# Weights of an input projection kept by column block instead of by half of the contraction, with B21 as the second of seven products

## The chip, the cores and the metric

The kernel runs on one core of a Trainium2 chip. The metric is the device time of one execution in microseconds (us). The kernel before takes 1280.05 us, the median of three runs (1279.63 to 1282.67).

## The reference, cut to what matters

The kernel is one step of a decoder layer with two branches (causal pooling and a Mamba-2 scan) that share one input projection. The change touches the making of this projection for the prompt:

```python
h = rmsnorm(x, norm_g) * (1 + scale[:, None]) + shift[:, None]   # 1024 x 1024
proj = h @ w_in
u_pool, z_pool, z_ssm, xbc, dt_raw, g_raw = jnp.split(proj, SPLITS, axis=-1)
...
xbc_c, conv_new = causal_conv(xbc, conv_buf, conv_w, conv_b)
dt = jax.nn.softplus(dt_raw.astype(jnp.float32) + dt_bias.astype(jnp.float32))
```

All inputs and outputs are 32-bit floats. w_in has 1024 rows, the contraction. dt_raw and one pair of the gates' column blocks are made apart, ahead of the rest; the other columns go through the code of the change.

## The kernel before, in words

**The tiling.** The columns of w_in are worked through in blocks of 128, two at a time. There are 31 such pairs. In 23 of them the two blocks are neighbours, in the other 8 they lie apart. A pair is a matrix product of a 1024-wide contraction with 256 columns, over 1024 tokens, and is done by one step of the Strassen-Winograd scheme: the contraction and the columns are cut in halves, so that the raw weights of a pair are four blocks of 512 x 128, held as tiles of 128 partitions x 512 numbers: B11 and B12 (upper half of the contraction, first and second column block), B21 and B22 (lower half). Seven products take the place of eight. Their weights are B11, B21, B22 and four combinations, in the names of the code:

- t3 = B22 - B12
- t2 = t3 + B11
- B12 - B11, written over B12
- t2 - B21, the weight of the seventh product (the change names it t4)

The operands on the side of the tokens (S1 to S4 and plain parts of h) are made once, before the pairs.

**High and low halves.** Each weight is split by `split` (L162) into a high half `whi`, which ScalarE copies with rounding (L165), and a low half `wlo`, which GpSimd subtracts (L168; VectorE in the very first pair). Both have four buffers. A product (`product`, L596) is 24 matmuls of 128 x 272: two halves of the tokens, three terms (high by high, high by low, low by high), four slices of the contraction. High halves of the weight are read in the first eight of twelve, the low half in the last four. A half of the tokens ends in a bank of TensorE's output (PSUM, tiles `mm` and `ps`), and VectorE or ScalarE empties it with the function given to `product` (lines 614, 619 and 646 are these: add to a running sum, put a result out, copy).

**The buffers.** The raw weights live in three buffers `rawA`. A pair takes two: the first load holds B11 and B12, the second B21 and B22, each 512 KB (L537). Where the column blocks lie apart, each half is brought by two loads of 256 KB (L540). t3 and t2 take two of three buffers `raw`, made by `raw_`. The differences run on VectorE but for t2 - B21, which GpSimd does; all have line 551, in `diff`.

**The order of the work.** `pair_w` (L529) issues the loads and makes the first weight (B11), and leaves the others to a generator `steps`. `run_units` calls it one pair ahead of its use. `between(n)` (L699) runs behind product n of a pair, counted from 0, and for n = 3, 4 and 5 it does the next of the three steps of the following pair: first t3, then t2 and its splits, then the rest. So most pairs have their weights ready before their first product. What is left of the steps when a pair starts is done at once (`run` in `pair`, L670). Three pairs stand out:

- The first pair has an order of its own (`first_steps`, `opening`), with B21 as second product already.
- The second pair starts right behind the first one, which has no `between`. All three steps of the second pair are run at its start.
- The last ten pairs are a second call of `run_units` (L1688). There is no pair ahead within that call, so the first of the ten also runs all its steps at its start. In that stretch `samples_beside` (L1651) lets the chain that makes dt run beside the products: dt goes out to DRAM, comes back as the tile s (L1080, on the SP queue) and is turned by TensorE (L1099). From there on the order of TensorE's instructions is that of the program.

The framework then orders the instructions of each engine by a simulated schedule with priorities; each engine runs its own in that order, and the queue of SP issues most loads in its order. A load waits in the SP queue until its buffer is free, and what is behind it waits too. Along with the pairs the queue stores scratch weights (`ws`, L438), and VectorE runs the convolution (`GA`, L1047).

```python
def fourth(s, p):
    out(d1, HF, u3, c2)(s, p)
    add(u2, u2)(s, p)
```

The running sums of a pair are s1, u2, u3 and the scratch c2, each with 2 x 272 numbers on a partition. `out` writes a finished quarter of the pair's result, with a buffer of that set as the place for it.

Of the kernel before, what the change touches and what calls it, by code (L numbers as in the profile page):

```python
# [8 lines left out]
F32 = mybir.dt.float32  # L9
# [11 lines left out]
P = 128  # L21
D = 1024
KT = D // P
# [18 lines left out]
HF, SB = T // 2, T // 4  # L42
# [4 lines left out]
def tile_pool_ssd_step(  # L47
# [6 lines left out]
    nc = tc.nc  # L54
    uid = [0]

    def nm(s):
        uid[0] += 1
        return f"{s}_{uid[0]}"
# [10 lines left out]
    def open_(name, bufs, side="left"):  # L70
        cm = tc.tile_pool(name=name, bufs=bufs, side=side, reuse_waits="tile")
        kept.append(cm)
        return cm.__enter__()
# [10 lines left out]
    pa = open_("pa", 1)  # L84
# [25 lines left out]
    load = nc.sync.dma_start  # L110
# [60 lines left out]
    def raw_(shape=(P, 4, P)):  # L171
        return pa.tile(list(shape), F32, tag="raw", name=nm("raw"), bufs=RAW)
# [291 lines left out]
    S2, S1, S3 = [None] * 4, [None] * 4, [None] * 4  # L464

    def a_part(i, j):
        sl = lambda s: slice(HF * i + SB * s, HF * i + SB * s + SB)
        return lambda k, s: (hh_[4 * j + k][:, sl(s)], hl_[4 * j + k][:, sl(s)])

    def s_part(lst):  # L470
        return lambda k, s: (lst[k][:, 0, SB * s:SB * s + SB], lst[k][:, 1, SB * s:SB * s + SB])
# [57 lines left out]
    def pair_w(c0, c1, pri, early):  # L529
        def run():  # L530
            with tc.high_priority(pri):
                raws = []
                for j in range(2):
                    r = pa.tile([P, 4, 2, P], F32, tag="rawA", name=nm("rawA"), bufs=3)
                    rows_ = w_in[0, j * 512:(j + 1) * 512]
                    if c1 == c0 + P:
                        load(r, rows_[:, c0:c0 + 2 * P].rearrange("(k p) (t c) -> p k t c", p=P, c=P))  # L537
                    else:
                        for t, c in enumerate((c0, c1)):
                            load(r[:, :, t], rows_[:, c:c + P].rearrange("(k p) c -> p k c", p=P))  # L540
                    raws.append(r)
            b11, b12, b21, b22 = raws[0][:, :, 0], raws[0][:, :, 1], raws[1][:, :, 0], raws[1][:, :, 1]
            w = []

            def add(x):
                with tc.high_priority(pri):
                    w.append(split(x, highs, eng=V if early else None))

            def diff(dst, x, y, op=ALU.subtract, eng=V):
                with tc.high_priority(pri):  # L550
                    eng.tensor_tensor(dst, x, y, op)  # L551

            def first_steps():
                t3, t2 = raw_(), raw_()
                diff(t3, b22, b12)
                diff(t2, t3, b11, ALU.add)
                yield
                add(b11)
                add(b21)
                diff(b21, t2, b21)  # L560
                yield
                add(b21)
                add(t2)
                yield
                add(t3)
                yield
                diff(b12, b12, b11)
                add(b12)
                yield
                add(b22)  # L570
                yield

            def steps():
                t3, t2 = raw_(), raw_()
                diff(t3, b22, b12)
                yield
                diff(t2, t3, b11, ALU.add)
                add(t2)
                add(t3)
                yield  # L580
                diff(b12, b12, b11)
                add(b12)
                add(b21)
                diff(t2, t2, b21, eng=nc.gpsimd)
                add(t2)
                add(b22)
                yield
            if early:
                return w, first_steps()
            add(b11)  # L590
            prep_q.append(steps())
            return w, prep_q[-1]
        return run
# [4 lines left out]
    def product(w, A, use):  # L598
        for s in range(2):
            turn[0] ^= 1  # L600
            p = (PA if turn[0] else PB)()[:, :SB]

            for j in range(12):
                k = j % 4
                mm(p, w[j // 8][:, k], A(k, s)[j // 4 == 1], start=(j == 0), stop=(j == 11))  # L605
            with tc.high_priority(PRI):
                use(s, p)

    def strassen(w, d0, d1, early=False):
        def tmp(tag):  # L610
            return pa.tile([P, 2, SB], F32, tag=tag, name=nm(tag))

        def add(x, y):
            return lambda s, p: V.tensor_tensor(y[:, s], x[:, s], p, ALU.add)  # L614

        def out(d, o, x, buf, op=ALU.add):
            def use(s, p):
                def put(dst, a=0, b=SB, v=lambda t: t):
                    V.tensor_tensor(dst, v(x[:, s, a:b]), v(p[:, a:b]), op)
                d(o + SB * s, SB, put, buf)  # L620
            return use

        def fourth(s, p):
            out(d1, HF, u3, c2)(s, p)
            add(u2, u2)(s, p)
        s1, u2, u3, c2 = tmp("s1"), tmp("u2"), tmp("u3"), tmp("c2")
        if early:
            def fifth(s, p):
                out(d0, HF, s1, u3, ALU.subtract)(s, u3[:, s])
                out(d1, HF, s1, c2)(s, p)  # L630
                add(u2, u2)(s, p)
            product(w[0], a_part(0, 0), lambda s, p: act(s1[:, s], p, AF.Copy))
            yield
            product(w[1], a_part(0, 1), out(d0, 0, s1, c2))
            yield
            product(w[2], a_part(1, 1), lambda s, p: act(u3[:, s], p, AF.Copy))
            yield
            product(w[3], s_part(S2), add(s1, u2))
            yield
            product(w[4], s_part(S3), add(u2, s1))  # L640
            yield
            product(w[5], s_part(S1), fifth)
            yield
            product(w[6], s4_part, out(d1, 0, u2, u2))
            return
        product(w[0], a_part(0, 0), lambda s, p: act(s1[:, s], p, AF.Copy))
        yield
        product(w[1], s_part(S2), add(s1, u2))
        yield
        product(w[2], s_part(S3), add(u2, u3))  # L650
        yield
        product(w[3], s_part(S1), fourth)
        yield
        product(w[4], a_part(0, 1), out(d0, 0, s1, s1))
        yield
        product(w[5], a_part(1, 1), out(d0, HF, u3, u3, ALU.subtract))
        yield
        product(w[6], s4_part, out(d1, 0, u2, u2))
# [1283 lines left out]
    for half in range(2):  # L1942
        c = slice(half * 512, half * 512 + 512)
# [32 lines left out]
    for i in range(8):  # L1976
# [4 lines left out]
        r = R((P, D))  # L1981
# [5 lines left out]
        out = y_prompt[0, i * P:(i + 1) * P, :]  # L1987
        for j, (c0, cw) in enumerate(cuts):
            s = slice(c0, c0 + cw)
# [57 lines left out]
```

## Time and profile before

| what | value |
|---|---|
| median of three runs | 1280.05 us (1279.63 to 1282.67) |
| the profiled execution's own time | 1281.91 us |
| its span, from the first to the last instruction | 1280.2 us |
| granted clock of TensorE, mean | 0.997 |
| busy: TensorE (PE) | 1255.5 us, 98% of the span |
| busy: VectorE (DVE), ScalarE (ACT), GpSimd (POOL) | 911.1, 657.0, 645.7 us |
| moved by DMA | 251.68 MB |

How to read the rows below. PE, DVE, ACT and POOL are the engines TensorE, VectorE, ScalarE and GpSimd; SPq is the DMA queue that SyncE issues. A row of the timeline has the start (us from the span's start), the length from there to the end of the group, the engine, the line of the program, the operation, `out<-in` by the program's names, the shapes, and xN for N instructions in a row; in brackets stands the idle time just before, with what ended it. A row of the windows has the stretch and its length, then for TensorE's matmuls, TensorE's weight loads, VectorE, ScalarE and GpSimd the number of instructions and the busy time, then the granted clock, the DMA share, and GB/s. A row of the waits has the waiting engine, tile and line, an arrow to what it waited for, and the sum, count and mean in us. A row of a tile has the engine, the operation, the count, the shortest, mean and longest duration in ns, and the stretch of the program. A row of a DMA queue has packets, MB and the share of the 16 DMA engines' time in the stretch.

### The profile page before, as it was taken

The numbers are of one execution on the slowest core, as the hardware profiler recorded it, in microseconds if no ns is written. First come the engines' busy times: TensorE is split into PE (matmuls) and PEld (weight loads), VectorE is DVE, ScalarE is ACT, GpSimd is POOL, SyncE is SP. The second block draws the span as 40 slices with busy tenths as digits, with TensorE's granted clock in tenths as the row PEclk, the third lists the DMA queues.
The fourth block names the chain that finished last, engine by engine and source line by source line (L and its number), as shares of the span: only waits on it lengthen the run. The fifth ranks groups of instructions, "written<-read, shape, count | busy, mean of one in ns | idle before, by whom it ended". The sixth has DMA issues, their size and how long they took to land.

```text
span 1280.2 us, 26308 instructions
## 1 busy us (share of the span) xinstructions
PE 1255.5 (98%) x9739; PEld 1172.3 (92%) x9739; DVE 911.1 (71%) x1635; ACT 657.0 (51%) x1508; POOL 645.7 (50%) x556
## 2 busy tenths in 40 slices
PE   7999999999999999999999999999999999999997
PEld 6779999999999999999999999989888889999786
DVE  4686678986989688776666665587766887579343
ACT  4665347465656555555656554655675756202111
POOL 1006659777868677554444444355666867300000
PEclk9999999999999999999999999999999999999999
DMA  9736354465456544444656564999769898675531
GB/s 332 244 118 210 121 172 155 152 209 186 135 170 209 160 151 147 136 162 126 179 166 197 158 192 143 336 323 299 229 216 277 271 297 261 211 265 183 210 107 50
DMA packets 232769, 251.68 MB, mean 197 GB/s; under 512 B 29729, under 2 KB 176881, under 8 KB 232634
## 3 DMA queue, kind: packets, MB, share of 16 engines
q1 hardware_dynamic: 160544, 171.60, 43.0%
q10 hardware_dynamic: 72098, 78.41, 18.0%
q8 instruction: 77, 1.26, 0.4%
q14 instruction: 50, 0.41, 0.1%
HBM read 167.06 MB, written 83.01 MB: 195 GB/s over the span
## 4 chain that ended last, share of the span: by engine, by line
PE 90%; DMA 3%; DVE 3%; ACT 2%; issue 2%; POOL 0%; ACTq 0%; SPq 0%; DVEq 0%; POOLq 0%
PE ps L605 23%; PE mm L605 23%; PE mm L358 19%; PE ps L1204 3%; PE ps L1993 2%; PE ps L1995 2%; PE ps L1994 2%; PE pc L1526 2%; PE ps L1207 2%; PE ps L233 2%; PE ps L1501 1%; PE ps L1294 1%; PE ps L1317 1%; DMA rawA<-in_w_in 1%; PE pc L1308 1%
## 5 line engine op out<-in xcount | busy, mean ns | idle before, releaser
L168 POOL TENSOR_TENSOR wlo<-rawA,whi 128x512 fp32r<-128x512 f32 x120 | 178.1, 1489 | 174.6 <-ACT whi L165 83.6
L168 POOL TENSOR_TENSOR wlo<-raw,whi 128x512 fp32r<-128x512 f32 x92 | 149.2, 1631 | 118.1 <-ACT whi L165 87.4
L358 PE MATMUL mm<-Y,whi 128*128 128x352 f32 (+1 forms) x960 | 197.0, 336 | 0.3 <-DVE Y L1564 0.3
L358 PEld LDWEIGHTS mm<-Y,whi 128*128 128x128 f32 x960 | 160.2, 189 | 6.5 <-issue 4.8
L605 PE MATMUL mm<-Y,whi 128*128 128x272 f32 x992 | 149.7, 293 | 2.2 <-ACT whi L165 2.2
L605 PE MATMUL ps<-Y,whi 128*128 128x272 f32 x992 | 145.7, 289 | 0.0
L605 PEld LDWEIGHTS mm<-Y,whi 128*128 128x128 f32 x992 | 133.5, 189 | 5.9 <-ACT whi L165 2.5
L605 PEld LDWEIGHTS ps<-Y,whi 128*128 128x128 f32 x992 | 132.7, 188 | 0.5 <-issue 0.4
L1047 DVE SCALAR_TENSOR_TENSOR GA<-GA,cvT,GA 128x1112 f32<-128x1112 f32 x72 | 129.2, 1798 | 0.4 <-ACT GA L1044 0.3
L165 ACT ACTIVATE whi<-rawA 128x512 fp32r<-128x512 f32 x125 | 78.3, 627 | 86.6 <-PE ps L605 55.8
L165 ACT ACTIVATE whi<-raw 128x512 fp32r<-128x512 f32 x96 | 58.5, 627 | 99.2 <-DVE raw L551 40.2
L358 PE MATMUL mm<-Y,wlo 128*128 128x352 f32 (+1 forms) x480 | 99.7, 329 | 0.0
L1192 ACT ACTIVATE dec<-dec,acT 128x128 f32<-128x128 f32 (+1 forms) x288 | 86.7, 383 | 23.1 <-POOL dec L1183 22.5
L605 PE MATMUL mm<-Y,wlo 128*128 128x272 f32 x496 | 84.2, 289 | 0.0
L605 PE MATMUL ps<-Y,wlo 128*128 128x272 f32 x496 | 82.7, 289 | 0.0
L358 PEld LDWEIGHTS mm<-Y,wlo 128*128 128x128 f32 x480 | 82.4, 189 | 0.1
L605 PE MATMUL mm<-G,whi 128*128 128x272 f32 x496 | 73.1, 290 | 1.2 <-DVE u L614 1.2
L605 PE MATMUL ps<-G,whi 128*128 128x272 f32 x496 | 72.7, 288 | 1.0 <-DVE u L614 1.0
L434 POOL TENSOR_TENSOR pw<-pw,ph 128x512 fp32r<-128x512 f32 x40 | 62.5, 1563 | 21.5 <-ACT ph L432 20.0
L605 PEld LDWEIGHTS mm<-Y,wlo 128*128 128x128 f32 x496 | 70.3, 188 | 0.4 <-POOL wlo L168 0.3
L605 PEld LDWEIGHTS ps<-Y,wlo 128*128 128x128 f32 x496 | 70.0, 188 | 0.0
L605 PEld LDWEIGHTS mm<-G,whi 128*128 128x128 f32 x496 | 66.5, 189 | 2.0 <-issue 1.3
(429 smaller groups left out, 2909.8 us busy)
## 6 DMA issues: line engine op xcount, KB each, us to landing
rawA<-in_w_in SPq DMA_DIRECT2D x46, 512.0 KB
dec<-acs_d SPq DMA_DIRECT2D x32, 512.0 KB
xbc<-GA ACTq DMA_DIRECT2D x24, 512.0 KB
rawA<-in_w_in SPq DMA_DIRECT2D x32, 256.0 KB
pw<-in_w_ssm_out ACTq DMA_DIRECT2D x32, 256.0 KB
ws<-ph ACTq DMA_DIRECT2D x32, 256.0 KB
ws<-pw SPq DMA_DIRECT2D x32, 256.0 KB
h<-in_state_ssm SPq DMA_DIRECT2D x32, 256.0 KB
```

The source lines that it names most:

```text
L165: ins = act(hi[:, :, :ncols], raw[:, :, :ncols], AF.Copy)
L168: (eng or nc.gpsimd).tensor_tensor(lo[:, :, :ncols], raw[:, :, :ncols], hi[:, :, :ncols].bitcast(F32), ALU.subtract)
L233: mm(px[:, c:c + n], xt[:n, k * P:(k + 1) * P], dg[0][:n, i * P:i * P + n], start=True, stop=True)
L358: mm(ps[:, :n], w[k // 4][h][:, k % 4, :], r[k][:, o:o + n], start=(j == 0), stop=(j == len(terms) - 1))
L434: nc.gpsimd.tensor_tensor(raw.bitcast(F32R), raw, hi.bitcast(F32), ALU.subtract)
L605: mm(p, w[j // 8][:, k], A(k, s)[j // 4 == 1], start=(j == 0), stop=(j == 11))
L1047: V.scalar_tensor_tensor(d[:, :n], rp[:, k:k + n], cvT[:, 24 * k + mc:24 * k + mc + 1], d[:, :n], ALU.mult, ALU.add)
L1192: act(dec[:, h], dec[:, h], AF.Exp, bias=acT[:S, c, 8 * g + h:8 * g + h + 1], scale=-1.0)
L1204: mm(o[hh], xd[:S, 2 * q + hh, :], dec[:S, 2 * q + hh], start=True, stop=state is None)
L1207: mm(o[hh], state[:, h * 64:h * 64 + 64], cE[:, h], start=False, stop=True)
L1526: mm(pu, bt, xw.rearrange("p h d -> p (h d)"), start=True, stop=True)
L1993: mm(ps[:, :cw], mhk, wo[k][0][:, s], start=(k == 0), stop=False)
```

## The change

It does three things.

- **Buffers by column block.** A buffer rawA now holds one column block over the whole contraction: the first B11 and B21, the second B12 and B22. There are two loads of 512 KB for every pair, also where the blocks lie apart, and each row of a load is a run of 128 numbers (512 bytes). Before, neighbouring blocks came in runs of 256 numbers.
- **The order of the products.** The products of every pair but the first were B11, t2, t3, B12 - B11, B21, B22, t2 - B21. They are now B11, B21, t2, t3, B12 - B11, B22, t4 = t2 - B21. The places of c2 and s1 in the running sums are exchanged to suit.
- **The steps.** The first step is t3 as before. The second makes t2, then the weights B21, t2 and t3 and the difference t4. The third makes B12 - B11 and its weight, and the weights t4 and B22. t4 has a buffer `raw` of its own, the third, where it was written over t2.

```diff
-                raws = []
-                for j in range(2):
-                    r = pa.tile([P, 4, 2, P], F32, tag="rawA", name=nm("rawA"), bufs=3)
-                    rows_ = w_in[0, j * 512:(j + 1) * 512]
-                    if c1 == c0 + P:
-                        load(r, rows_[:, c0:c0 + 2 * P].rearrange("(k p) (t c) -> p k t c", p=P, c=P))
-                    else:
-                        for t, c in enumerate((c0, c1)):
-                            load(r[:, :, t], rows_[:, c:c + P].rearrange("(k p) c -> p k c", p=P))
-                    raws.append(r)
-            b11, b12, b21, b22 = raws[0][:, :, 0], raws[0][:, :, 1], raws[1][:, :, 0], raws[1][:, :, 1]
+                cols = []
+                for c in (c0, c1):
+                    r = pa.tile([P, KT, P], F32, tag="rawA", name=nm("rawA"), bufs=3)
+                    load(r, w_in[0, :, c:c + P].rearrange("(k p) c -> p k c", p=P))
+                    cols.append(r)
+            (b11, b21), (b12, b22) = [(r[:, 0:4], r[:, 4:8]) for r in cols]
...
                 diff(t3, b22, b12)
                 yield
+
                 diff(t2, t3, b11, ALU.add)
+                t4 = raw_()
+                add(b21)
                 add(t2)
                 add(t3)
+                diff(t4, t2, b21, eng=nc.gpsimd)
                 yield
                 diff(b12, b12, b11)
                 add(b12)
-                add(b21)
-                diff(t2, t2, b21, eng=nc.gpsimd)
-                add(t2)
+                add(t4)
                 add(b22)
                 yield
...
         def fourth(s, p):
-            out(d1, HF, u3, c2)(s, p)
+            out(d1, HF, u3, s1)(s, p)
             add(u2, u2)(s, p)
...
-        product(w[1], s_part(S2), add(s1, u2))
-        yield
-        product(w[2], s_part(S3), add(u2, u3))
-        yield
-        product(w[3], s_part(S1), fourth)
-        yield
-        product(w[4], a_part(0, 1), out(d0, 0, s1, s1))
+        product(w[1], a_part(0, 1), out(d0, 0, s1, c2))
+        yield
+        product(w[2], s_part(S2), add(s1, u2))
+        yield
+        product(w[3], s_part(S3), add(u2, u3))
+        yield
+        product(w[4], s_part(S1), fourth)
         yield
```

Behind the change every line of the program stands three lines earlier, so that L165 and L168 stay and L605, L614, L619, L646, L1047, L1080 and L1099 become L602, L611, L616, L643, L1044, L1077 and L1096. The loads are then L535 and the differences L546.

How the instructions move on three engines, at the places that the prediction speaks of. A row has the line, the operation, and `out<-in` with the number of each buffer's use.

ScalarE where the second pair starts, before. rawA_1310 is B11 of the next pair, rawA_1302 the upper half of the second pair; raw_1325 is its t2 and raw_1324 its t3.

```order
L165 ACTIVATE whi_1316<-rawA_1310 128x512
L715 ACTIVATE u_133_1039<-u_133_1039 128x272
L646 ACTIVATE s_186_1354<-mm_1358 128x272
L432 ACTIVATE ph_1480<-pw_1386 128x512
L717 DMA z_166<-u_133_1039 128x544
L715 ACTIVATE c_134_1040<-c_134_1040 128x272
L433 DMA wp_178<-ph_1480 128x512
L717 DMA z_166<-c_134_1040 128x544
L715 ACTIVATE u_132_1038<-u_132_1038 128x272 x2
L165 ACTIVATE whi_1328<-raw_1325 128x512
L165 ACTIVATE whi_1332<-raw_1324 128x512
```

The same place now. rawA_1302 is the first column block of the second pair, and its copy in the second row is that of B21; raw_1323 is t2 and raw_1322 t3.

```order
L165 ACTIVATE whi_1314<-rawA_1310 128x512
L165 ACTIVATE whi_1327<-rawA_1302 128x512
L712 ACTIVATE u_133_1039<-u_133_1039 128x272
L643 ACTIVATE s_187_1353<-mm_1357 128x272
L432 ACTIVATE ph_1477<-pw_1385 128x512
L165 ACTIVATE whi_1331<-raw_1323 128x512
L714 DMA z_166<-u_133_1039 128x544
L712 ACTIVATE c_134_1040<-c_134_1040 128x272
L165 ACTIVATE whi_1335<-raw_1322 128x512
```

The copy for the second product (t2) stood nine rows behind that of the next pair's B11. The copy for the second product (now B21) stands right behind it, and that of t2 five rows behind.

VectorE at the same place, before. L484 makes the low halves of the tokens' operand Y for the last product of the first pair, L619 and L614 empty its banks.

```order
L168 TENSOR_TENSOR wlo_1222<-rawA_717,whi_1221 128x512
L484 TENSOR_TENSOR Y_486<-tf_323,Y_485 128x544
L484 TENSOR_TENSOR Y_486<-tf_328,Y_485 128x544
L619 TENSOR_TENSOR u_133_1039<-s_131_1037,u_133_1039 128x272
L619 TENSOR_TENSOR c_134_1040<-s_131_1037,mm_1229 128x272
L614 TENSOR_TENSOR u_132_1038<-u_132_1038,mm_1229 128x272
L619 TENSOR_TENSOR u_133_1039<-s_131_1037,u_133_1039 128x272
L619 TENSOR_TENSOR c_134_1040<-s_131_1037,ps_1247 128x272
L614 TENSOR_TENSOR u_132_1038<-u_132_1038,ps_1247 128x272
L551 TENSOR_TENSOR raw_1324<-rawA_1304,rawA_1302 128x512
```

And now:

```order
L168 TENSOR_TENSOR wlo_1222<-rawA_717,whi_1221 128x512
L546 TENSOR_TENSOR raw_1322<-rawA_1304 128x512
L484 TENSOR_TENSOR Y_486<-tf_323,Y_485 128x544
L484 TENSOR_TENSOR Y_486<-tf_328,Y_485 128x544
L616 TENSOR_TENSOR u_133_1039<-s_131_1037,u_133_1039 128x272
```

The difference t3 of the second pair has moved from behind the six operations on the banks to ahead of the last two low halves of Y.

The SP queue where the last ten pairs start, before. rawA_7472 and rawA_7474 are the two loads of the first of the ten, rawA_7480 and rawA_7482 those of the next pair.

```order
L438 DMA ws_214<-pw_6728 128x512
L438 DMA ws_215<-pw_6865 128x512
L537 DMA rawA_7472<-in_w_in 128x4x256
L438 DMA ws_216<-pw_7040 128x512
L438 DMA ws_217<-pw_7177 128x512
L537 DMA rawA_7474<-in_w_in 128x4x256
L537 DMA rawA_7480<-in_w_in 128x4x256
L537 DMA rawA_7482<-in_w_in 128x4x256
L1080 DMA s_7466<-dts_d 128x1024
```

And now, where rawA_7476 and rawA_7478 are the first of the ten:

```order
L438 DMA ws_214<-pw_6727 128x512
L438 DMA ws_215<-pw_6868 128x512
L438 DMA ws_216<-pw_7040 128x512
L535 DMA rawA_7476<-in_w_in 128x8x128
L438 DMA ws_217<-pw_7181 128x512
L535 DMA rawA_7478<-in_w_in 128x8x128
L535 DMA rawA_7484<-in_w_in 128x8x128
L535 DMA rawA_7486<-in_w_in 128x8x128
L1077 DMA s_7470<-dts_d 128x1024
```

The first load has changed places with one store of scratch; the second load stands behind the same stores as before, and the load of s behind the same loads.

## The prediction

> **What bounds the kernel now.** I read the page first: busy times, and the chain of waits that ended last.
>
> ```profile
> span 1280.2 us, 26308 instructions
> ...
> PE 1255.5 (98%) x9739; PEld 1172.3 (92%) x9739; DVE 911.1 (71%) x1635; ACT 657.0 (51%) x1508; POOL 645.7 (50%) x556
> ...
> PE 90%; DMA 3%; DVE 3%; ACT 2%; issue 2%; POOL 0%; ACTq 0%; SPq 0%; DVEq 0%; POOLq 0%
> ```
>
> TensorE is busy for 1255.5 of 1280.2 us and makes up 90% of the chain. The change adds and removes no matmul, so it can only win or lose TensorE's idle time, 24.7 us in the whole program. The pairs of column blocks, which the change touches, run from about 80 to 815 us. The windows and TensorE's waits in that stretch:
>
> ```profile
> 120.00:500.00 380.00, 380.00 (x2978) 373.86 (x2978) 306.88 (x470) 210.13 (x498) 281.51 (x173) 1.00 0.52 166
> ```
>
> ```profile
> PE mm L605 <- ACT whi L165: 2.2, 1, 2.2
> PE ps L1099 <- DMA s<-dts_d: 1.6, 1, 1.6
> PE mm L605 <- DVE u L614: 1.2, 1, 1.2
> PE ps L605 <- DVE u L614: 1.0, 1, 1.0
> PE ps L1317 <- ACT s L646: 0.9, 2, 0.6
> PE ps L1264 <- DVE u L614: 0.4, 1, 0.4
> ```
>
> From 120 to 500 us TensorE never stops: 2978 matmuls in 380 us, 127.6 ns each, so a product (24 matmuls) is about 3.1 us. All recorded waits of the stretch are 2.2 + 1.6 + 1.2 + 1.0 + 0.9 + 0.4 = 7.3 us. That is the most that the change can give. The first four, 6.0 us, stand at two places: where the second pair starts, and where the last ten pairs start. Exactly there a pair's weights are made all at once just before use, not a pair ahead. I then read the timeline at both.
>
> **The second pair (99 to 108 us).** The timeline, all engines:
>
> ```profile
> 99.50 2.46 DVE L484 TENSOR_TENSOR Y<-tf,Y 128x544 fp32r<-128x544 f32 x2
> ...
> 102.03 0.37 PE L605 MATMUL mm<-Y,whi 128*128 128x272 f32 x1
> ...
> 103.17 0.61 ACT L165 ACTIVATE whi<-rawA 128x512 fp32r<-128x512 f32 x1
> ...
> 103.98 1.79 DVE L551 TENSOR_TENSOR raw<-rawA,rawA 128x512 f32<-128x512 f32 x1
> ...
> 107.48 1.15 ACT L165 ACTIVATE whi<-raw 128x512 fp32r<-128x512 f32 x2 [0.56 <-DVE raw L551]
> 108.17 1.27 PE L605 MATMUL mm<-Y,whi 128*128 128x272 f32 x8 [2.24 <-ACT whi L165]
> ```
>
> The second product of this pair takes t2, which needs two differences on VectorE; the first starts at 103.98, and the copy whi comes at 107.48. TensorE waits 2.24 us for it. In the change the second product takes B21, which needs no difference. Its copy stands in ScalarE's order right behind the copy of 103.17 (the next pair's b11), so it would be there at 103.17 + 0.61 + 0.61 = 104.4, about 1.5 us before TensorE asks at 108.17 - 2.24 = 105.9. The third product (t2) is asked for a product later. **Term 1: -2.24 us.** What would be late next is that copy at 103.17: it waits for a load issued at 99.6, now one of 512 KB and not two of 256 KB. A load of 512 KB was released 4.04 us after its issue in the case below (531.41 to 535.45), so 103.65 instead of 103.17, inside the 1.5 us.
>
> Something is given back here. In VectorE's order the first difference now stands ahead of the two subtractions of 99.50 (L484), the low halves that the last product of the first pair reads. They end at 101.96 and the matmul of 102.03 starts at once: no slack. Durations of such operations:
>
> ```profile
> L168 POOL TENSOR_TENSOR wlo<-rawA,whi x120: 1267/1297/2379, 99.6 to 802.5; 128x512 fp32r<-128x512 f32 x120
> ...
> L551 DVE TENSOR_TENSOR raw<-rawA,rawA x31: 677/1337/2346, 50.2 to 783.2; 128x512 f32<-128x512 f32 x31
> ...
> L551 POOL TENSOR_TENSOR raw<-raw,rawA x30: 1280/1332/2383, 112.0 to 792.1; 128x512 f32<-128x512 f32 x30
> ```
>
> A difference takes 0.68 us undisturbed and 1.79 us in the slow case seen at 103.98. VectorE has to do the two low halves either way, and they already ran slowly there (2.46 for two), so I take the undisturbed price. **Term 2: +0.7 us, between 0 and 1.8.** On this the Trainium skill, "SBUF — State Buffer", section "Who interferes with whom", says that a VectorE instruction with two SBUF inputs and a GpSimd instruction that reads SBUF exclude each other for a whole instruction. The row's 677 against 2346 ns agrees. By that rule one GpSimd instruction of 1.3 us is in the way of the whole block once, as before, which gives the same +0.7.
>
> **The last ten pairs (522 to 562 us).**
>
> ```profile
> 522.54 1.77 DVE L551 TENSOR_TENSOR rawA<-rawA 128x512 f32<-128x512 f32 x1
> ...
> 528.90 0.42 DVE L614 TENSOR_TENSOR u<-s,mm 128x272 f32<-128x272 f32 x1
> ...
> 530.09 2.54 POOL L168 TENSOR_TENSOR wlo<-rawA,whi 128x512 fp32r<-128x512 f32 x2
> ...
> 531.41 4.14 SPq L537 DMA_DIRECT2D rawA<-in_w_in  x2
> ...
> 535.45 1.75 DVE L551 TENSOR_TENSOR raw<-rawA,rawA 128x512 f32<-128x512 f32 x1 [6.13 <-DMA rawA<-in_w_in]
> ...
> 537.13 0.42 DVE L614 TENSOR_TENSOR u<-s,ps 128x272 f32<-128x272 f32 x1
> 537.61 1.28 PE L605 MATMUL ps<-G,whi 128*128 128x272 f32 x8 [1.02 <-DVE u L614]
> ...
> 540.54 1.23 PE L605 MATMUL mm<-G,whi 128*128 128x272 f32 x8 [1.15 <-DVE u L614]
> ```
>
> VectorE stands 6.13 us before a difference whose operand is still being loaded. The load is late because its buffer holds the previous pair's upper half, B11 and B12. It is free only when GpSimd has made the low half of B12 - B11 (530.09), which is the fourth weight and waits for the pair before to end. Behind VectorE's wait stand the operations that empty TensorE's banks (537.13), and TensorE loses 1.02 + 1.15 us.
>
> In the change the second load of a pair takes the buffer of the previous pair's first column. B11 and B21 are used up by the difference of 522.54, the second copy and one subtraction on GpSimd, all in the steps behind the fifth and sixth product of the pair before. So the load can go at 522.54 + 1.77 = 524.3, or when the SP queue has stored the scratch that is ahead of it in both orders. With 4.04 us it lands at 528.4, when VectorE gets there (528.9, less one operation of 0.42 that now comes later). What is late next: all three differences now stand together ahead of the two operations that empty the banks, 3 x 0.68 to 3 x 1.79, 2.0 to 5.4 us. The bank of 537.61 was wanted at 537.61 - 1.02 = 536.6; the change has emptied it by 528.5 + 5.4 + 2 x 0.42 = 534.7 at the latest. **Term 3: -2.17 us.**
>
> The same queue holds the third place:
>
> ```profile
> 554.93 0.37 SPq L537 DMA_DIRECT2D rawA<-in_w_in  x1
> ...
> 555.47 0.38 SPq L1080 DMA_DIRECT2D s<-dts_d  x1
> ...
> 559.10 0.66 PE L605 MATMUL mm<-G,whi 128*128 128x272 f32 x4
> 561.31 1.09 PE L1099 MATMUL ps<-ident,s 128*128 128x128 f32 x8 [1.56 <-DMA s<-dts_d]
> ```
>
> The load s is queued behind the next pair's second load, which again waits for a buffer until 554.93. In the change that buffer is free after the copy and low half of B21, the second weight and not the fourth: two products, about 6 us, sooner. TensorE reaches L1099 only some 1 us sooner by its order. **Term 4: -1.56 us, between -1.56 and 0.**
>
> **What costs nothing.** The loads: all are now 512 KB in runs of 512 bytes, where 46 of them had runs of 1 KB. The same amount in both forms, from the DMA view of one stretch of 3.6 us and one of 3.8 us:
>
> ```profile
> q1 hardware_dynamic: 1056, 0.52, 52.4%
> ```
>
> ```profile
> q1 hardware_dynamic: 528, 0.52, 47.0%
> ```
>
> That is 0.524 x 16 x 3.6 = 30.2 us of engine time against 0.470 x 16 x 3.8 = 28.6, or 0.1 us per load over 16 engines. The DMA share in the windows row is 0.52, so it is hidden; uncovered it would cost 0.1 us at each of the two waited-for loads. The Trainium skill speaks against the change here: "DMA: Bandwidth & Descriptors", section "Why small descriptors are slow (HBM only)", gives a packet a fixed extra of about 3 cycles. By it 512 bytes cost 19 cycles and 1 KB 35, an estimate of 9% more, against 6% measured; the sum would be the same to 0.1 us. The eight pairs with columns apart issue two loads instead of four, and shorten the SP queue. Swapping c2 and s1 moves as many VectorE and ScalarE operations as before. The third piece of work per pair takes the third raw buffer; its owner in the next pair comes a whole pair later.
>
> The steady pairs: GpSimd's order was low halves of t2 and t3, then the subtraction; now it is low half of B21, subtraction, low half of t2. So t2's low half is put back by 2.6 to 4.8 us (one low half and one subtraction), and its product by 3.1: the margin changes by between +0.5 and -1.7 us. A pair of the heavy stretch:
>
> ```profile
> 411.06 3.97 POOL L168 TENSOR_TENSOR wlo<-raw,whi 128x512 fp32r<-128x512 f32 x2 [1.41 <-issue]
> ...
> 415.51 0.41 PE L605 MATMUL mm<-Y,wlo 128*128 128x272 f32 x2
> ```
>
> The first of the two is done by 413.4 and read at 415.51: 2.1 us of margin, more than 1.7. B21 no longer waits for VectorE either. Price taken: 0.
>
> **Sum.** -2.24 + 0.70 - 2.17 - 1.56 = -5.27 us. The profiled execution took 1281.91 us (span 1280.2), 1.86 above the median of the runs, 1280.05; its sum gives 1276.6. Taken off the median: 1274.8 us.
>
> **Rivals.** (1) The queue keeps it: SP gives the load s no earlier, because the copy of B21 itself sits late in ScalarE's order. Term 4 is 0: -3.7, 1276.3 us. Against it: the copy of B21 is now the second weight to be made, not the fifth; for it: ScalarE runs its queue in order. (2) The wait changes its place: the load of 524.3 is held by the scratch store ahead of it, and VectorE waits in front of its three differences. From a landing later than 536.6 - 0.84 - 5.4 = 530.4 on, TensorE waits again; at the old 535.45 terms 3 and 4 are gone: -1.5, 1278.5 us. (3) Slower: GpSimd. It is busy 281.51 of 380 us. If most of the 19 steady pairs up to 520 us have a margin under 1.2 us for t2's low half, not the 2.1 quoted, each loses about 0.5 us: +9.5 - 5.3 = +4.2, 1284.3 us. For it: GpSimd's long cases (2379 ns); against it: not one wait for wlo among TensorE's waits today.
>
> **How the numbers follow.** A measurement of this kernel tells about 0.3%, 3.8 us, from no change; faster is below 1276.2, slower above 1283.9. Forecast 0.50; rival 1 0.15; rival 2 0.23; rival 3 0.12. The forecast counts as faster nearly whole (0.48), and rival 1 sits at the bound, mostly inside (0.04 faster), which makes 0.52; rivals 1 and 2 with the forecast's remainder give 0.36 for the same; slower 0.12. All of the 7.3 us gone and term 2 at nothing gives 1272.8 as the low end. The high end is rival 2 with term 2 at 1.8 and a further 1 us, half the wait of term 3, behind the block of three: 1280.6. That leaves out rival 3 and little else.
>
> **What would show it.** Right: the waits of TensorE between 80 and 815 us lose the rows for ACT whi, DVE u and DMA s, and keep about 1.3 us; VectorE's 6.1 us for the load of rawA are gone; a new small wait or pause of 0.7 us stands near 102 us. Wrong: waits of TensorE for POOL wlo in the steady pairs (rival 3), VectorE waiting for rawA near 527 us (rival 2), or L1096 waiting for s (rival 1). A gain elsewhere than in these rows would make the argument wrong even at the right time.

## The result, and the profile after

The changed kernel takes 1290.67 us (median of 6 runs, 1289.49 to 1292.61) against 1280.68 us for the kernel before (median of 6). The ratio is 1.0075, with a 95% interval of 1.0062 to 1.0089: 10 us slower, where 5 us faster was forecast. In what follows, one execution of e11 that took 4936.75 us is left out of its ratio.

Three slips in the text above change no number of it. The weight t2 - B21 (t4) is the sixth of the seven and B22 the seventh, in both kernels. A row of a tile has the shortest, the median and the longest duration, not the mean. And a row of the waits has the sum, the count and the longest wait, not the mean.

The page of the changed kernel: its span and busy times.

```profile
span 1289.7 us, 26396 instructions
...
PE 1257.6 (98%) x9739; PEld 1172.6 (91%) x9739; DVE 925.9 (72%) x1635; ACT 657.8 (51%) x1508; POOL 645.2 (50%) x556
```

VectorE is busy 14.8 us longer (925.9 against 911.1) with the same 1635 instructions. TensorE's waits while the pairs run, from 80 to 815 us (sum, count, longest):

```profile
PE ps L1314 <- ACT s L643: 4.3, 2, 2.7
PE ps L806 <- DVE GA L790: 2.5, 1, 2.5
PE ps L1150 <- DVE wdT L1140: 1.3, 1, 1.3
PE ps L1201 <- DVE u L611: 1.3, 1, 1.3
PE ps L1263 <- DVE tn L1331: 1.3, 2, 0.6
PE ps L806 <- DVE u L611: 1.1, 1, 1.1
PE mm L602 <- DVE Y L484: 1.0, 2, 0.8
PE mm L602 <- DVE c L616: 0.9, 1, 0.9
PE ps L602 <- DVE GA L616: 0.4, 1, 0.4
```

Of the 7.3 us of before, the rows for ACT whi, DMA s and the two for DVE u in the products are gone, as forecast. But the rows now add up to 14.1 us, and 11.8 of these stand at other lines than the product's, where 2.9 us stood before (0.9 + 0.4 + 1.6): L806 is the product of the pooling branch, and L1150, L1201, L1263 and L1314 belong to the samples, whose work TensorE does between the products of the last ten pairs. The clock adds to this. Two windows of the changed kernel, behind the waits that end at 259.49 and at 751.01 us (the granted clock is the third number from the end):

```profile
260.00:264.00 4.00, 4.00 (x17) 3.40 (x17) 3.19 (x7) 3.87 (x9) 2.58 (x3) 0.57 0.44 109
752.00:755.00 3.00, 3.00 (x15) 3.00 (x15) 1.20 (x5) 0.00 (x0) 0.03 (x1) 0.50 0.75 238
```

It is 0.57 and 0.50 there. The clock record has it at a half for 3.41 us each time, from 260.20 and from 751.72 us on, which costs about 1.7 us twice. In the kernel before, no such stretch lies among the pairs; it has one behind them, at 1124.59 us, which the changed kernel's profile has not. Waits and clock of the pairs together: 14.1 - 7.3 + 3.4 = 10.2 us. Less 1.7 us for the later stretch that is gone, 8.5 us are left, against 9.5 us by which the span grew; 0.7 us of the rest is idle time of TensorE outside the pairs. So most of the loss lies in the pairs' stretch, and most of that in waits of TensorE's other work.

How two of these waits arise, from the timeline. In the eighth pair, ScalarE (first and second row) copies the weight t4, for which a buffer whi is free only when the second product has ended, ahead of the second half of s, the first product's result:

```profile
244.43 0.63 ACT L165 ACTIVATE whi<-raw 128x512 fp32r<-128x512 f32 x1 [0.97 <-PE ps L602]
244.97 0.38 ACT L643 ACTIVATE s<-ps 128x272 f32<-128x272 f32 x1
...
245.38 0.44 DVE L616 TENSOR_TENSOR GA<-s,ps 128x272 f32<-128x272 f32 x1 [3.46 <-ACT s L643]
...
256.02 1.24 DVE L789 TENSOR_TENSOR edge<-GA,rc 128x7 f32<-128x7 f32 x1
...
259.49 1.93 PE L806 MATMUL ps<-GA,pwt 128*128 128x256 f32 x4 [2.53 <-DVE GA L790]
```

VectorE needs s to empty the second product's banks, stands 3.46 us, and does not catch up before TensorE asks for the pooled rows at L806. On the way an operation on 7 numbers (L789) takes 1.24 us; e8 comes back to it. Among the samples, one chain of lateness goes through VectorE and ScalarE:

```profile
649.04 3.28 DVE L546 TENSOR_TENSOR rawA<-rawA,rawA 128x512 f32<-128x512 f32 x1
652.25 2.14 DVE L1317 SCALAR_TENSOR_TENSOR h<-h,E,ps 128x128 f32<-128x128 f32 x8
...
653.88 1.28 ACT L1189 ACT_TABLE_LOAD   x1 [2.78 <-DVE h L1317]
...
657.73 1.28 ACT L712 ACT_TABLE_LOAD   x1
659.03 0.75 ACT L712 ACTIVATE u<-u 128x272 f32<-128x272 f32 x2
659.68 0.38 ACT L643 ACTIVATE s<-mm 128x272 f32<-128x272 f32 x1
660.20 0.63 ACT L165 ACTIVATE whi<-rawA 128x512 fp32r<-128x512 f32 x1
660.73 0.38 ACT L643 ACTIVATE s<-ps 128x272 f32<-128x272 f32 x1
...
661.17 0.50 PE L1314 MATMUL ps<-dec 96*128 96x512 f32 x1 [2.68 <-ACT s L643]
```

The difference B12 - B11 takes 3.28 us, the states h come late, ScalarE stands 2.78 us for them, and the copy s, which would free the bank for L1314, stands behind a table load, sigmoids and a weight's copy.

### The profile page after: what moved, and what is told of

It reads as the page before. It is cut to its first block, busy times and chain, and to the rows that moved or that the text cites. A ratio compares the mean times of both kernels' runs of the same rounds, so it can differ in the third digit from the quotient of the medians.

```text
span 1289.7 us, 26396 instructions
## 1 busy us (share of the span) xinstructions
PE 1257.6 (98%) x9739; PEld 1172.6 (91%) x9739; DVE 925.9 (72%) x1635; ACT 657.8 (51%) x1508; POOL 645.2 (50%) x556
## 4 chain that ended last, share of the span: by engine, by line
PE 55%; DVE 4%; DMA 2%; issue 1%; ACT 1%; ACTq 0%; SPq 0%; POOL 0%; DVEq 0%; POOLq 0%
PE mm L358 18%; PE ps L602 9%; PE mm L602 9%; PE ps L1201 3%; PE ps L1990 2%; PE ps L1991 2%; PE ps L1992 2%; PE pc L1523 2%; PE ps L1204 2%; PE ps L1498 1%; DVE GA L1044 1%; PE ps L1291 1%; PE ps L1314 1%; DMA bc<-xbc 1%; PE pc L1305 1%
## 5 line engine op out<-in xcount | busy, mean ns | idle before, releaser
L168 POOL TENSOR_TENSOR wlo<-rawA,whi 128x512 fp32r<-128x512 f32 x120 | 179.3, 1501 | 205.8 <-ACT whi L165 112.9
L168 POOL TENSOR_TENSOR wlo<-raw,whi 128x512 fp32r<-128x512 f32 x92 | 150.0, 1636 | 92.6 <-ACT whi L165 67.5
L602 PE MATMUL mm<-Y,whi 128*128 128x272 f32 x992 | 151.7, 294 | 1.1 <-DVE Y L484 1.0
L602 PE MATMUL ps<-Y,whi 128*128 128x272 f32 x992 | 145.7, 289 | 0.0
L602 PEld LDWEIGHTS mm<-Y,whi 128*128 128x128 f32 x992 | 133.8, 190 | 5.4 <-DVE Y L484 1.4
L602 PEld LDWEIGHTS ps<-Y,whi 128*128 128x128 f32 x992 | 132.7, 188 | 0.6 <-issue 0.4
L1044 DVE SCALAR_TENSOR_TENSOR GA<-GA,cvT,GA 128x1112 f32<-128x1112 f32 x72 | 127.1, 1770 | 0.1
L165 ACT ACTIVATE whi<-rawA 128x512 fp32r<-128x512 f32 x125 | 78.0, 627 | 81.9 <-PE ps L602 62.4
L165 ACT ACTIVATE whi<-raw 128x512 fp32r<-128x512 f32 x96 | 59.9, 626 | 93.2 <-PE ps L602 40.2
L602 PE MATMUL mm<-Y,wlo 128*128 128x272 f32 x496 | 82.8, 289 | 0.0
L602 PE MATMUL ps<-Y,wlo 128*128 128x272 f32 x496 | 82.7, 288 | 0.0
L434 POOL TENSOR_TENSOR pw<-pw,ph 128x512 fp32r<-128x512 f32 x40 | 67.7, 1692 | 17.5 <-ACT ph L432 17.4
L602 PE MATMUL mm<-G,whi 128*128 128x272 f32 x496 | 74.3, 291 | 0.0
L602 PE MATMUL ps<-G,whi 128*128 128x272 f32 x496 | 73.4, 291 | 0.4 <-DVE GA L616 0.4
L602 PEld LDWEIGHTS mm<-Y,wlo 128*128 128x128 f32 x496 | 70.0, 189 | 0.1
L602 PEld LDWEIGHTS ps<-Y,wlo 128*128 128x128 f32 x496 | 70.0, 188 | 0.0
L602 PEld LDWEIGHTS mm<-G,whi 128*128 128x128 f32 x496 | 67.2, 190 | 0.6
```

The lines of the kernel that those rows point to most:

```text
L165: ins = act(hi[:, :, :ncols], raw[:, :, :ncols], AF.Copy)
L168: (eng or nc.gpsimd).tensor_tensor(lo[:, :, :ncols], raw[:, :, :ncols], hi[:, :, :ncols].bitcast(F32), ALU.subtract)
L434: nc.gpsimd.tensor_tensor(raw.bitcast(F32R), raw, hi.bitcast(F32), ALU.subtract)
L1044: V.scalar_tensor_tensor(d[:, :n], rp[:, k:k + n], cvT[:, 24 * k + mc:24 * k + mc + 1], d[:, :n], ALU.mult, ALU.add)
```

## The experiments

Two theories were set against each other. **A:** the new order of the products costs the time, since it shifts the emptying of banks and the copies on ScalarE and VectorE for which TensorE's other work waits. **B:** the layout costs it, since VectorE's differences got slower (the three groups of L551 and L546 that write raw or rawA: 105.4 us before, 123.9 after). Kernels are compared by their ratio to runs of the kernel before that were made along with each.

**Each part alone.** e1 takes the loads of the changed kernel and leaves order and steps; e2 takes order and steps, and leaves the loads.

```diff
 e1: before with
-                raws = []  ...  load(r, rows_[:, c0:c0 + 2 * P]...)
+                cols = []  ...  load(r, w_in[0, :, c:c + P]...)
 e2: after with the loads of before
```

> Buffers by column block alone, with the old order of the products and the old steps. Theory A (the new order of the products costs the time: it moves the work that empties the banks and the copies on ScalarE): this kernel keeps the old order and should take 1277 to 1282 us, with the 2.2 us wait of TensorE for whi at the second pair still there and no new waits of 1 us or more in the side work of the last ten pairs. Theory B (the layout makes VectorE's differences slower, 123.9 us in all after against 105.4 before, and VectorE comes late everywhere): 1286 us or more, and the differences take about 120 us here too.

> The new order of the products and the new steps alone, with buffers by half of the contraction as before. Theory A (order): 1286 to 1292 us, with waits of TensorE for ScalarE's copy s in the last ten pairs as in the changed kernel (4.3 us there). Theory B (layout): 1275 to 1281 us, differences near 105 us on VectorE.

e1: 1284.27 us, ratio 1.0035 (1.0023 to 1.0047). e2: 1287.50 us, ratio 1.0065 (1.0052 to 1.0077). TensorE's waits in e2, the largest:

```profile
PE ps L1319 <- ACT s L648: 3.1, 2, 1.6
PE ps L1031 <- DVE u L621: 2.4, 2, 1.4
PE mm L607 <- DVE u L616: 1.5, 1, 1.5
PE ps L1155 <- DVE wdT L1145: 1.3, 1, 1.3
PE ps L1268 <- DVE tn L1336: 1.3, 2, 0.6
```

The order alone brings most of the loss, and three of the four waits in the samples' work (L1319, L1155 and L1268 are L1314, L1150 and L1263 of the changed kernel; L1201 has no counterpart here). The slow differences come with the order too: 117.3 us in e2 (37.3 + 39.8 + 40.2), 98.9 in e1. So theory B has the wrong cause for them. But A's number for e1 was missed: the layout costs 4.4 us in the old order by the medians (0.35%). VectorE's waits for loads in e1, and the same row of the changed kernel:

```profile
DVE raw L546 <- DMA rawA<-in_w_in: 15.9, 8, 4.9
```

```profile
DVE raw L546 <- DMA rawA<-in_w_in: 2.3, 2, 1.7
```

Before it was one wait of 6.1 us. With the old order, B21 is used up late, by the last subtraction on GpSimd, and now it holds the buffer that the next pair's second load needs. That reading is argued from the code and the rows; it was not tried by itself. Nor does it say where TensorE loses the time: in e1's profiled execution (1282.56 us) TensorE's waits among the pairs add up to 7.4 us, no more than the 7.3 us before, and one stretch at half clock (from 655.05 us, about 1.7 us lost) is the only other loss that it shows there. In the changed kernel that wait is small, and whether the layout adds to the loss there is not settled: 1.0065 and 1.0075 have overlapping intervals.

**Which engine is late.** e3 moves the copy s of the last ten pairs to VectorE, e5 that of all pairs but the first; e4 moves t4 to VectorE.

```diff
 e3: after with
-        product(w[0], a_part(0, 0), lambda s, p: act(s1[:, s], p, AF.Copy))
+        product(w[0], a_part(0, 0), (lambda s, p: V.tensor_copy(s1[:, s], p)) if late[0] else (lambda s, p: act(s1[:, s], p, AF.Copy)))
 e5: after with
+        product(w[0], a_part(0, 0), lambda s, p: V.tensor_copy(s1[:, s], p))
 e4: after with
-                diff(t4, t2, b21, eng=nc.gpsimd)
+                diff(t4, t2, b21)
```

> The changed kernel, with the first product of each of the last ten pairs copied out of its banks by VectorE and not by ScalarE. Theory A says the waits of 2.68 and 1.59 us before L1314, and the stretch of 3.4 us at half clock after the second (1.7 us), come from ScalarE's queue, in which the copy stands behind sigmoids, a table load and a weight's copy: they go, 6.0 us, and the time is 1284 to 1287 us. If VectorE is what is late everywhere (theory B), twenty more copies on it (20 x 0.4 us) make it the same or slower: 1290 to 1294 us.

> The changed kernel, with the difference t4 on VectorE and not on GpSimd. Theory B (VectorE's differences are held up by GpSimd's instructions on the same buffers): the 93 differences of before lose part of their 123.9 us and the time falls to 1288 us or less, though 30 differences of 0.7 us are added. Theory A: VectorE only gets more to do, 1290 to 1295 us.

> The changed kernel, with the first product of every pair but the very first copied by VectorE. TensorE's order is all but that of the changed kernel. Theory A: the wait of 2.5 us at 259 us, with the 3.4 us at half clock behind it, comes from one copy s on ScalarE that stands behind a weight's copy which waits for the end of the second product (VectorE then stands 3.46 us for s). It goes too: against the kernel with VectorE's copies in the last ten pairs only (1285.7 us) 2 to 4 us less, 1281 to 1284 us, and VectorE's waits for s (28 us in all) are gone. Theory B (VectorE's load): 42 copies of 0.43 us more, 18 us, on a VectorE that is 80% busy in the heavy pairs: 1287 us or more, with longer waits before the pooled product L806.

e3: 1285.72 us, ratio 1.0047 (1.0035 to 1.0059). That is 0.28%, about 3.6 us, less than the changed kernel by the ratios (4.95 us by the medians). TensorE's order in its trace is that of the changed kernel, row for row. Its waits from 560 to 815 us:

```profile
PE ps L1150 <- DVE wdT L1140: 1.3, 1, 1.3
PE ps L1263 <- DVE tn L1331: 1.2, 2, 0.6
PE ps L1201 <- DVE u L611: 1.2, 1, 1.2
```

The row for ACT s is gone and the others stand. So the copy's place in ScalarE's queue is what TensorE waits for there (e8, below, shows that VectorE's lateness has a part in it too). e4: 1292.81 us, 1.0107 (1.0092 to 1.0122): taking GpSimd's subtraction to VectorE makes it worse, as A said. e5: 1289.32 us, 1.0071 (1.0059 to 1.0083), a miss for A. The wait at the eighth pair fell from 2.53 to 0.92 us, but in an earlier pair the pooled product now waits 2.27 us, and L1201 waits 2.19 us: VectorE has no room for 40 copies more than in e3 (20 pairs of two; the 42 of the expectation is a miscount). In the heavy pairs VectorE's load counts as well as ScalarE's order.

**With no side work.** In e6 the samples' work is taken out from between the products and done in one block near the end of the ten pairs, in both kernels.

```diff
-        while made_[0] < (due[0] - FIRST) * 4 * SSTEPS / (7 * LAST - FIRST - SPARE):
+        while made_[0] < (4 * SSTEPS + 1 if due[0] >= 7 * LAST - SPARE else 0):
```

> The kernel before, with the side work of the samples taken out from between the products of the last ten pairs and done in one block near their end. It is the base of the next run: the seven pairs from the 24th to the 30th run with no side work between their products. All theories: TensorE has no wait over 0.3 us in those pairs; the whole time is longer, since the block waits for its own chain.

> The changed kernel with the same move. Theory A (the new order costs only where side work on TensorE waits for operations that the new order puts later on ScalarE and VectorE): from the start of the 24th pair to the start of the 29th it takes the same time as the kernel before with the same move, within 0.5 us. Rival C (the new order slows the pairs themselves, by banks emptied later or weights made later): it takes 2 us or more longer there too.

Windows of the two kernels with the move, first before, then after:

```profile
640.00:740.00 100.00, 100.00 (x799) 100.00 (x798) 42.43 (x84) 39.43 (x79) 49.91 (x38) 1.00 0.30 97
```

```profile
640.00:740.00 100.00, 100.00 (x799) 100.00 (x799) 44.86 (x78) 38.57 (x81) 49.69 (x38) 1.00 0.33 100
```

And the two as they were, in a stretch of 150 us, first before, then after:

```profile
600.00:750.00 150.00, 148.68 (x1338) 140.72 (x1337) 97.83 (x247) 90.03 (x192) 67.56 (x56) 1.00 0.60 178
```

```profile
600.00:750.00 150.00, 144.23 (x1288) 136.34 (x1286) 101.76 (x235) 85.72 (x184) 66.03 (x54) 1.00 0.58 167
```

Without side work both do 799 matmuls in 100 us and never stop. With it TensorE stands 1.3 us before and 5.8 us after. In these pairs the new order does not slow the products; it makes the side work between them wait. For the heavy pairs e6 shows nothing of the kind: the waits before L806 stand in it too (2.6 and 0.8 us), and so does the wait of 1.3 us before L1150, at 598 us. The whole times of these two runs (1340.98 and 1345.72 us, one run each) are longer because the block waits for its own chain; the changed kernel is still the slower one, by 4.7 us.

**The slow differences.** e8 gives the low half of B21 to VectorE.

```diff
-                add(b21)
+                add(b21, True)   # True: low half on VectorE
...
```

> The changed kernel, with the low half of B21 made by VectorE and not by GpSimd. Theory D on the slow differences (t2's difference takes 1.34 us in the mean after and 0.88 before, because GpSimd now makes the low half of B21 at that moment, and the two hold each other up): t2's difference falls back to 0.9 us in the mean, and the three differences from 123.9 us in all to about 110. The time stays within 1288 to 1292 us, since VectorE gets 30 low halves of 0.7 us for the 14 us. Rival: another GpSimd instruction takes that place, and the mean stays at 1.2 us or more.

The difference t2 = t3 + B11 before, after and in e8 (shortest, median, longest in ns):

```profile
L551 DVE TENSOR_TENSOR raw<-raw,rawA x31: 673/684/1790, 50.9 to 787.3; 128x512 f32<-128x512 f32 x31
```

```profile
L546 DVE TENSOR_TENSOR raw<-raw,rawA x31: 676/1610/2594, 50.6 to 798.6; 128x512 f32<-128x512 f32 x31
```

```profile
L546 DVE TENSOR_TENSOR raw<-raw,rawA x31: 675/683/1790, 50.6 to 792.7; 128x512 f32<-128x512 f32 x31
```

The median goes from 684 to 1610 ns and back to 683. In the traces, GpSimd makes a low half from rawA during 4 of the 31 differences before, 21 after and 2 in e8. Where no GpSimd instruction ran beside it, the difference never took more than 692 ns in any of the three. That is the price of the new steps: B21 needs no difference, so its low half starts at once, just when VectorE makes t2. The Trainium skill, "SBUF — State Buffer", section "Who interferes with whom", says that VectorE shares a pair of ports with GpSimd and that the lock is exclusive; the three rows agree with it. The three differences went from 123.9 to 105.0 us (35.1 + 43.2 + 26.7), and the kernel to 1285.76 us, ratio 1.0059 (1.0043 to 1.0076). By the median that is better than the forecast of 1288 to 1292 us; by the ratio it is 0.16% less than the changed kernel, and the two intervals overlap, so the gain in time is not clear of noise. The waits changed more plainly. That before L1314 fell from 4.3 to 0.9 us, though the copy s stayed on ScalarE. That of 2.53 us before L806 fell to 0.2, though VectorE still stands 2.95 us for s in the eighth pair; the operation on 7 numbers takes

```profile
254.94 0.15 DVE L789 TENSOR_TENSOR edge<-GA,rc 128x7 f32<-128x7 f32 x1
```

where it took 1.24 us beside a GpSimd low half. So VectorE's lateness beside GpSimd has a part in both waits, along with ScalarE's order.

e11 makes both moves, e3 and e8.

> The changed kernel with both moves: the low half of B21 on VectorE, and the first product of the last ten pairs copied by VectorE. Alone they gave 4.9 and 5.0 us. The first has already taken most of the wait before L1314 (4.3 us to 0.9), so the two overlap: 1283.5 to 1286 us. If they were apart, 1280.8 us.

1284.22 us, ratio 1.0032 (1.0020 to 1.0045). The median lies in the range, but the overlap is not shown: by the ratios the moves gave 0.28% and 0.16% alone and 0.43% together, which is their sum. Together they take back a good half of the 0.75%.

**The change only where it was wanted.** e7 is the kernel before with the new order in the second pair and the first of the last ten alone. e9 keeps it in the second pair alone and moves the copy s of the last ten pairs to VectorE. e10 is e9 with the column layout.

```diff
+    QUICK = (C_Z + 2 * P, C_Z + 10 * P)      # e9, e10: (C_Z + 2 * P,)
...
-            prep_q.append(steps())
+            prep_q.append(quick_steps() if c0 in QUICK else steps())
...
+        if quick:   # the order of the changed kernel
...
```

> The kernel before with the new order of products and steps only in the second pair and in the first of the last ten pairs, and buffers by half as before. Theory A: the waits at those two places go (2.24 us at the second pair, part of the 2.17 and 1.56 us at the last ten) and the new waits in the heavy pairs and the side work do not come: 1275 to 1278.5 us, 1.5 to 5 us faster than before. Rival: any new schedule brings waits of its own, whatever is changed: 1280 to 1285 us.

> The kernel before with the new order of products and steps in the second pair alone, buffers by half, and the first product of the last ten pairs copied by VectorE. Theory A: at the last ten pairs the waits are those of before (2.2 + 1.6 us), not those of the run with two changed pairs (1.15 + 2.56 us and 1.7 us of half clock), the two small waits for s there (0.9 us) go, and the second pair keeps its gain: 1274.5 to 1277.5 us. Rival (any new schedule brings waits of its own): 1278 us or more.

> The kernel of the run with the second pair alone in the new order, with buffers by column block in every pair. If the layout costs by itself (its own run was 4.4 us slower in the median, but only 0.7 us in its profiled execution), this kernel takes 1279 to 1282 us; if what it cost there was that schedule's, 1276 to 1278 us.

e7: 1278.02 us, ratio 0.9985 (0.9976 to 0.9993). The time lies in A's range. At the second pair the 2.24 us are gone. At the last ten pairs it lost what it should have won: one wait is longer, and the clock falls behind it. So the rival, that a new schedule brings waits of its own, has a part here.

```profile
548.18 1.37 PE L623 MATMUL mm<-G,whi 128*128 128x272 f32 x8 [2.56 <-ACT whi L165]
...
549.00:552.00 3.00, 3.00 (x15) 2.68 (x14) 0.00 (x0) 2.00 (x5) 1.78 (x2) 0.54 0.92 348
```

e9: 1276.88 us, ratio 0.9984 (0.9975 to 0.9992), 2.3 us faster than before, though by less than the 0.3% named above, and not to be told from e7 by the ratios. It lies in A's range. Its waits of over 1 us are the three of the last ten pairs that were known from before:

```profile
PE mm L623 <- DVE u L632: 1.1, 1, 1.1
PE ps L1129 <- DMA s<-dts_d: 1.1, 1, 1.1
PE ps L623 <- DVE u L632: 1.0, 1, 1.0
```

e10: 1283.97 us, ratio 1.0035 (1.0022 to 1.0048), above both forecasts. Against e9 the layout costs 0.5%, and it cost 0.35% in e1, so with two schedules it costs time in the old order. VectorE's waits for loads are long in both: 16.4 us here against 8.3 us in e9, as 15.9 in e1 against 6.1.

## Why the prediction was wrong

- **Term 1** (-2.24 us) was right. The wait is gone in the changed kernel, and e7 and e9 show it gone by the second pair's own order.
- **Term 2** (+0.7, up to 1.8) came out at 1.0 us, the row for DVE Y L484, but near the forecast by luck:

```profile
101.09 0.69 DVE L546 TENSOR_TENSOR raw<-rawA 128x512 f32<-128x512 f32 x1 [1.74 <-DMA rawA<-in_w_in]
101.70 1.35 DVE L484 TENSOR_TENSOR Y<-tf,Y 128x544 fp32r<-128x544 f32 x2
...
102.48 0.39 PE L602 MATMUL mm<-Y,whi 128*128 128x272 f32 x1 [0.76 <-DVE Y L484]
```

  The difference takes 0.69 us, as priced, but VectorE first stands 1.74 us for its load, which the working did not have, and the two low halves of Y take 1.35 us in place of 2.46. The two errors partly cancel. The cost goes with the layout: e1 and e10 show the same order of VectorE and waits for Y of 0.6 and 0.7 us, and e2, e7 and e9, with buffers by half, show neither.
- **Term 3** (-2.17) was mis-sized, by a wrong step: that the second load could go at 524.3 us, when the difference of 522.54 was done. Three rows of the changed kernel:

```profile
530.78 1.74 POOL L546 TENSOR_TENSOR raw<-raw,rawA 128x512 f32<-128x512 f32 x1
...
532.54 12.63 SPq L535 DMA_DIRECT2D rawA<-in_w_in  x2
...
541.53 0.65 PE L602 MATMUL mm<-R,whi 128*128 128x272 f32 x3 [0.92 <-DVE c L616]
```

  The subtraction t4 on GpSimd is the last to read the buffer, it ends at 532.5, and the load goes then. Counted from the start of the pair ahead (522.67 us before, 528.18 us now), the load went at 8.7 us, was to go at 1.6, and goes at 4.4. The working named that subtraction and put no time on it. The block of three differences then makes VectorE late, as rival 2 had it, though for another reason than the store of scratch that rival 2 named. TensorE loses 0.92 us in place of 2.17: a gain of 1.25 us.
- **Term 4** (-1.56) was right, in its mechanism too: the row for DMA s is gone. Counted from the first product of the first of the ten pairs (546.63 us before, 550.66 us now), the load s goes 5.2 us sooner and TensorE reaches L1096 1.5 us sooner, where the working had about 6 and 1.
- Together these places gave -2.24 + 1.0 - 1.25 - 1.56 = -4.05 us, where -5.27 was forecast. Had nothing else changed, the gain would have been a little smaller than forecast and of the right sign.
- **The step that failed** is the part on what costs nothing. It said that swapping c2 and s1 moves as many VectorE and ScalarE operations as before, and took a price of 0 for the steady pairs. The count was right and the price was not. The working weighed only whether the weights are ready, and they were: no wait for wlo, as rival 3 would have had it, and no wait for whi is left in the list. It never asked who else waits for VectorE and ScalarE in the pairs. The order puts the low half of B21 on GpSimd beside t2 on VectorE (e8), and lets ScalarE's copies of weights and sigmoids stand ahead of copies that empty banks (e3). What pays is TensorE's other work: the samples between the products of the last ten pairs (shown by e6) and the pooled product in the heavy pairs. Its waits went from 1.3 us (without term 4's 1.6) to 11.8 us, and two stretches of half clock cost about 3.4 us more.
- No rival had this mechanism. Rival 3 had the right sign by another one.
- **What stays open:** the two moves of e11 take back 0.43 of 0.75%, and the rest was not taken apart. The waits at L1150, L1201 and L1263, some 3.9 us, stand in the changed kernel and in all runs with the new order in every pair and the side work in place (e2 lacks L1201). They belong to the samples' work, but what makes each late was not traced. Why the framework's schedule puts one copy ahead of another was not traced either.

## What to carry to other kernels

When steps are put in another order, list for each engine that they touch who else waits for it, and not only the consumers of the steps themselves: work with a fixed place in a full engine's order has no slack. An operand that needs no preparation starts its other operations earlier, and these can collide with what ran alone before. A change that helps at two places of a long loop is worth trying at those places alone; here that gave 0.15%, where the change everywhere cost 0.75%.

## What the runs showed of the hardware

- TensorE's clock halved behind some short stops and not behind others. It fell to a half for 3.41 us after stops of 1.59 and 2.53 us in the changed kernel and of 2.56 us in e7, but not after 2.68 us in the changed kernel at 661 us and not after 2.24 and 1.56 us in the kernel before. The Trainium skill, "TensorE: Matmul & The Clock Gate", section "Why this matters for your kernels", asks for no gaps over about 3 us; here 1.59 us was enough, and the measurement decides. The length of a stop alone does not tell. The two half stretches of the changed kernel start 491.52 us apart, which is 144 times 3.413 us. Laid out from them, a grid of 3.413 us cuts the stop of 2.68 us into 1.07 and 1.61. In the kernel before, whose stretches at 56.21 and 1124.59 us lie 313 steps apart, it cuts that of 2.24 us into 1.49 and 0.75. The stops of 1.59, 2.53 and 1.56 us lie whole in one step. So what may count is the part of a stop within one step. That is argued from these stops, and no exact bound comes out of them: 1.59 us was followed by half clock, 1.61 and 1.56 us were not.
- A GpSimd instruction beside it can more than double a VectorE operation on two SBUF operands: 684 ns in the median against 1610 for the difference t2, and 0.15 us against 1.24 for an operation on 7 numbers.
